# A hybrid encoder layer: level masks applied to the products of an inversion, the first up products in source order, split up weights in a pool of their own

## The chip, the cores and the metric

The kernel runs on one core of a Trainium2 chip. The metric is the device time of one execution in microseconds (us). Before the change it was 1162.3 us, the median of three runs (1160.35 to 1165.93). TensorE is called PE here, VectorE DVE, ScalarE ACT, GpSimd POOL and SyncE, which issues the DMAs, SP, as in the profile.

## The reference

One layer on 1024 tokens of width 1024: a combined input projection, a pooling group and a gated DeltaNet group side by side, an output projection, a squared-ReLU MLP of width 4096, and a last RMSNorm. What matters here, cut short:

```python
u = rms_norm(h, norm_mix)
proj = u @ w_in
pool_out = pool_mixer(proj[..., :P], w_pool, pool_scale)
qkv = causal_conv_silu(proj[..., P:P + 3 * G], conv_w)
gdn_out = gated_delta_net(...)          # lhs = I + strictly lower m; solves lhs against v and k
h = h + concatenate([pool_out, gdn_out]) @ w_out
u = rms_norm(h, norm_mlp)
h = h + square(relu(u @ w_up)) @ w_down
return rms_norm(h, norm_final)
```

## The kernel before

Tokens lie in eight tiles of 128, weights in blocks of 128 x 512. A float32 product is made of three matmuls on split operands: ACT casts an operand to its high half, DVE or POOL subtracts that to get the low half (`split`, line 951; `wh`/`wl` are the two halves of a weight, `th`/`tl` those of an activation operand), and `mm3` adds high x high, low x high and high x low.

**Order.** PE's instructions run in the order in which the program writes them. A planner interleaves dense work (input projection, convolution, output projection) with the chunk work by estimated due times. DVE, ACT, POOL and SP are put in order by the framework's scheduler, each engine by itself; within an engine everything then runs in that order, so a waiting instruction holds all that stand behind it.

**Chunks.** The DeltaNet works on 8 chunks of 128 tokens for 4 heads at once (tiles of 128 x 512). `invert` (line 573) inverts the unit lower triangular matrix by doubling: at level l, from 1 to 6, the blocks of size 2^l next to the diagonal are cut out of the matrix (`m1`, which is stored with ones on its diagonal) by a mask `lev[l]`, which has -1 in these blocks and 0 elsewhere. The cut-out `bl` is a POOL product (line 588), then PE multiplies it with the inverse so far (`px`), DVE adds the identity (`xx`, line 592), and PE multiplies `xx` with the inverse in both forms (`t`, `tt`). Level 0 takes two DVE operations (lines 578 and 579). At the same time DVE computes the convolution of the next projection tiles (`cy`, line 391) and POOL the low halves of input weights (`wl`, line 133).

**Up projection.** It goes by Strassen's scheme: 16 column pairs p of `w_up`, each with seven products i over half of the tokens and half of the depth. `up_load` (line 961) brings the 1 MB of a pair, `up_ready` (line 965) makes the sums of blocks for product i and splits them, `up_product` (line 1014) multiplies and evacuates, `combine` (line 1000) makes the seven operands of the down stage and stores them to DRAM (`hd`). The operands from the activations, TH[i] and TL[i], are made once: 1 and 2 by `turn_first`, the rest by `turn_second` (6 and 3), `operands_5`, `operands_7` and `operands_4` from the rows R[11], R[12], R[21], R[2], R[4], while the products of pairs 0 and 1 run. The list `order` (line 1048) says in which sequence; from pair 2 on it is 1, 6, 2, 5, 7, 3, 4. DVE makes the sums of blocks for pairs 0 and 1, POOL those of later pairs.

**Down projection.** Again seven products over the stored operands; `down_load` (line 1095) brings one or two weight blocks of 512 KB and an operand of `hd`, `down_ready` (line 1109) subtracts and splits. SP issues all loads and stores in one queue. Stores of the last pair are kept in the list `late` and issued after the first loads.

**Pools.** `ws` has the tags `raw` (3 buffers), `wh` and `wl` (5 each), used for nearly all split weights; `cp` has nine tiles "c" for the up stage's results; `wr2` holds the second weight of the down stage.

Of the kernel before, what the change touches and what calls it, by code (L numbers as in the profile page):

```python
# [28 lines left out]
def hybrid_trunk(ctx, tc, x, norm_mix, w_in, conv_w, w_pool, pool_scale, a_log, dt_bias,  # L29
# [218 lines left out]

    lev = []
    for l in range(7):  # L250
        b = 1 << l
        m = gp.tile([P, P], F16, name=f"lev{l}")
        nb = P // (2 * b)
        m3 = m.rearrange("p (n q) -> p n q", q=2 * b)
        G.memset(m3[:, :, 0:b], 0.0)
        G.memset(m3[:, :, b:2 * b], -1.0)

        G.affine_select(m3, m3, pattern=[[-2 * b, nb], [0, 2 * b]], compare_op=ALU.is_ge, fill=0.0, base=0,
                        channel_multiplier=1)
        G.affine_select(m3, m3, pattern=[[2 * b, nb], [0, 2 * b]], compare_op=ALU.is_gt, fill=0.0, base=b,  # L260
                        channel_multiplier=-1)
        lev.append(m)
# [310 lines left out]
    def invert(c, r):  # L573

        m1 = r["m1"]
        t, tt = gt("t", 3, F16), gt("tt", 3, F16)
        b0 = gt("bl", 2, F16)
        V.tensor_tensor(b0, m1, bc(lev[0]), op=ALU.mult)
        V.tensor_tensor(tt, b0, bc(ident_h), op=ALU.add)
        yield 1.0 * SLACK  # L580
        pt = bank()
        for h in range(NH):
            T.matmul(pt[:, h, :], tt[:, h, :], ident_h, start=True, stop=True)
        A.copy(t, pt)
        yield 0.9 * SLACK
        for l in range(1, 7):
            bl = gt("bl", 2, F16)
            G.tensor_tensor(bl, m1, bc(lev[l]), op=ALU.mult)  # L588
            px = bank()
            mm(px, bl, t)  # L590
            xx = gt("xx", dt=F16)
            V.tensor_tensor(xx, px, bc(ident), op=ALU.add)  # L592
# [260 lines left out]
    TH, TL = {}, {}  # L853
    u2c, u2p = opened(name="u2", bufs=1, side="right", reuse_waits="tile")
# [21 lines left out]
    wt[0] = [split_w(wov[:, k, :HALF], [P, HALF], V, *((w2p, "w2h", "w2l", 4, w2p, 6) if k >= 4 else (None, "wh", "wl", 5)))  # L876
# [6 lines left out]
    ys += norm_v(1, 1)  # L883
# [5 lines left out]
    R[12], R[2] = (u3(f"r{n}", F32) for n in (12, 2))  # L889
# [10 lines left out]

    def c_tile(nm):
        return cp.tile([P, HALF], F32, name=nm, tag="c")
# [30 lines left out]
    def operands_5():  # L933
        TH[5], TL[5] = (big_tile(f"t{m}5", [4, HALF], F32R) for m in "hl")
        parts_of(5, rows_of(11))

    def operands_7():

        for j in range(4):
            weighed(R[12][:, j, :], 4 + j, R[12][:, j, :])  # L940
        R[4] = [c_tile("r4") for _ in range(4)]
        for j in range(4):
            V.tensor_tensor(R[4][j], R[21][:, j, :], R[2][:, j, :], op=ALU.subtract)
        TH[7], TL[7] = u3("th7", F32R), big_tile("tl7", [4, HALF], F32R)
        parts_of(7, rows_of(12))
# [17 lines left out]

    def up_ready(p, i):

        r = raws[p]
        a11, a12, a21, a22 = r[:, :4, :P], r[:, 4:, :P], r[:, :4, P:], r[:, 4:, P:]
        eng = V if p < 2 else G
        if i == 1:
            eng.tensor_tensor(a21, a21, a22, op=ALU.add)  # L970
# [43 lines left out]
    def up_product(p, i, w):  # L1014
# [27 lines left out]
        else:  # L1042
# [5 lines left out]
    order = [(0, 1), (1, 1), lambda: turn_second(ys), (0, 2), (1, 2), operands_5, (0, 6), (1, 6), operands_7,  # L1048
             (0, 5), (1, 5), (0, 3), (1, 3), operands_4, (0, 7), (1, 7), (0, 4), (1, 4)]
# [20 lines left out]
    used = 0  # L1070
    for e in order:
# [11 lines left out]

    wrc, wr = opened(name="wr", bufs=4, side="right", reuse_waits="tile")
    xrc, xr = opened(name="xr", bufs=4, side="right", reuse_waits="tile")
    nfc, nf = opened(name="nf", bufs=1, side="right", reuse_waits="tile")
# [20 lines left out]

    def down_ready(i, s):
        x, w = raw_x.pop((i, s)), raw_w.pop((i, s))
        t = w[0]  # L1110
        if i == 5:
# [3 lines left out]
            V.tensor_tensor(t, w[0], w[1], op=ALU.subtract)  # L1115
# [52 lines left out]
    for n, (i, s) in enumerate(todo):  # L1168
# [3 lines left out]
        while late:  # L1172
            store(*late.pop(0))
# [50 lines left out]
```

## Time and profile before

| | |
|---|---|
| profiled execution | 1163.48 us |
| its span | 1161.8 us |
| mean granted TensorE clock | 0.987 |
| median of three runs | 1162.3 us |
| TensorE matmul busy | 1100.9 us, 95% |
| VectorE busy | 789.8 us, 68% |
| ScalarE busy | 601.5 us, 52% |
| GpSimd busy | 303.5 us, 26% |
| first of the up products starts | 515.0 us |
| 14th of the up products ends | 569.0 us |
| turn from up to down | about 843 us |

The span counts from the first to the last instruction. A row of a group has line, engine, operation, output and inputs, shape and count, then the busy time and the mean of one in ns, then the engine's idle time just before and what ended it. A row of the timeline has the start in us, the duration, and in brackets how long the engine stood idle before it and on what it waited. A wait row names who waited, on whom, the us in total, how often, and the longest. A row of a stretch begins with its bounds and its length.

### The profile page before, as it was taken

To read this page: it belongs to the slowest core of one execution; us is meant where nothing else is said; L and a number is where in the kernel's file an instruction comes from. 1 tells how busy PE (TensorE), PEld (TensorE's weight loads), DVE (VectorE), ACT (ScalarE), POOL (GpSimd) and SP (SyncE) were. 2 spreads that over 40 slices of the span, in tenths; PEclk is the share of its full clock that TensorE was granted. 3 is DMA by queue.
4 is the path that set the end of the run, shared out by engine and by line. 5 is a ranking of instruction groups with operands and counts; after the bars stand their busy time and mean duration, and the time that the engine had idled before them with its cause. 6 is when DMAs were issued, how large, how long until landed. Compare 5 with 4: busy or idle time off the path is not lost.

```text
span 1161.8 us, 15593 instructions
## 1 busy us (share of the span) xinstructions
PE 1100.9 (95%) x5606; PEld 893.6 (77%) x5606; DVE 789.8 (68%) x1240; ACT 601.5 (52%) x1113; POOL 303.5 (26%) x272
## 2 busy tenths in 40 slices
PE   6998999988998999997999999999989999999997
PEld 5776777767776787876788888888878888888886
DVE  5798688867879775669655555555465687466584
ACT  6666566564755555546554544454444334335353
POOL 6033365564755422000232313131100000000010
PEclk9999999998999999998999999999989999999999
DMA  5233121111223321120634343444298796265561
GB/s 161 82 98 121 56 59 41 55 52 40 55 60 118 109 65 55 37 73 18 209 133 166 128 162 137 156 144 146 89 373 298 270 393 224 94 199 194 186 215 73
DMA packets 93049, 155.24 MB, mean 134 GB/s; under 512 B 7782, under 2 KB 45739, under 8 KB 92971
## 3 DMA queue, kind: packets, MB, share of 16 engines
q1 hardware_dynamic: 92970, 154.24, 39.4%
q8 instruction: 44, 0.72, 0.3%
q14 instruction: 35, 0.28, 0.1%
HBM read 120.66 MB, written 33.55 MB: 133 GB/s over the span
## 4 chain that ended last, share of the span: by engine, by line
PE 70%; DVE 13%; ACT 3%; issue 2%; POOL 1%; DMA 1%; POOLq 0%; DVEq 0%; ACTq 0%
PE bank L44 52%; PE acc L44 18%; DVE cy L391 2%; DVE nxt L410 1%; DVE xx L592 1%; PE bank L48 1%; DVE wl L955 1%; DVE nxt L409 0%; DMA wu<-in_w_up_dram 0%; DVE r L908 0%; DVE tl L913 0%; ACT th L172 0%; DVE ul L173 0%; DMA raw<-in_w_out_dram 0%; DVE kn L533 0%
## 5 line engine op out<-in xcount | busy, mean ns | idle before, releaser
L44 PE MATMUL bank<-tl,wh 128*128 128x512 f32 x440 | 175.3, 398 | 5.8 <-DVE tl L913 5.8
L44 PE MATMUL bank<-th,wh 128*128 128x512 f32 x440 | 175.2, 398 | 0.3 <-ACT p L1024 0.3
L44 PE MATMUL bank<-th,wl 128*128 128x512 f32 x440 | 174.7, 397 | 0.0
L954 ACT CAST sh<-x 128x1024 fp32r<-128x1024 f32 x55 | 57.9, 1053 | 163.8 <-PE bank L44 155.1
L954 ACT CAST wh<-wu 128x512 fp32r<-128x512 f32 x110 | 68.0, 620 | 127.2 <-PE bank L44 120.7
L44 PE MATMUL bank<-th,sh 128*128 128x512 f32 x344 | 133.8, 389 | 0.0
L44 PE MATMUL bank<-th,sl 128*128 128x512 f32 x344 | 133.8, 389 | 0.0
L44 PE MATMUL bank<-tl,sh 128*128 128x512 f32 x344 | 133.8, 389 | 0.0
L44 PE MATMUL acc<-uh,wh 128*128 128x512 f32 x320 | 130.3, 407 | 1.6 <-DVE ul L173 0.9
L44 PE MATMUL acc<-ul,wh 128*128 128x512 f32 x320 | 129.3, 404 | 0.0
L44 PE MATMUL acc<-uh,wl 128*128 128x512 f32 x320 | 128.9, 403 | 0.0
L955 DVE TENSOR_TENSOR sl<-x,sh 128x1024 fp32r<-128x1024 f32 x55 | 67.3, 1224 | 89.5 <-ACT sh L954 89.4
L44 PEld LDWEIGHTS bank<-tl,wh 128*128 128x128 f32 x440 | 83.5, 190 | 26.8 <-DVE tl L913 7.8
L955 DVE TENSOR_TENSOR wl<-wu,wh 128x512 fp32r<-128x512 f32 x110 | 84.4, 768 | 28.4 <-ACT wh L954 26.8
L44 PEld LDWEIGHTS bank<-th,wh 128*128 128x128 f32 x440 | 83.3, 189 | 20.1 <-ACT p L1024 0.8
L44 PEld LDWEIGHTS bank<-th,wl 128*128 128x128 f32 x440 | 83.5, 190 | 19.3
L152 POOL TENSOR_TENSOR stf<-stf,mhalf 128x1 f32<-128x1 f32 x8 | 7.9, 998 | 327.3 <-DVE stf L1159 327.3
L588 POOL TENSOR_TENSOR bl<-m,lev 128x512 f16<-128x512 f16 x48 | 62.9, 1310 | 84.7 <-PE bank L44 72.3
L391 DVE SCALAR_TENSOR_TENSOR cy<-cr,cols,cy 128x512 f32<-128x512 f32 x72 | 73.2, 1022 | 9.0 <-ACT cy L389 8.4
L133 POOL TENSOR_TENSOR wl<-raw,wh 128x512 fp32r<-128x512 f32 x48 | 68.0, 1420 | 35.6 <-ACT wh L132 35.4
L44 PEld LDWEIGHTS bank<-th,sl 128*128 128x128 f32 x344 | 64.6, 188 | 13.5
L44 PEld LDWEIGHTS bank<-th,sh 128*128 128x128 f32 x344 | 64.5, 188 | 13.5
(336 smaller groups left out, 2365.4 us busy)
## 6 DMA issues: line engine op xcount, KB each, us to landing
w<-in_w_down_dram SPq DMA_DIRECT2D x72, 512.0 KB, 5.9
x<-hd SPq DMA_DIRECT2D x56, 512.0 KB, 3.5
raw<-in_w_in_dram SPq DMA_DIRECT2D x80, 256.0 KB, 2.7
wu<-in_w_up_dram SPq DMA_DIRECT2D x16, 1024.0 KB, 5.3
hd<-s SPq DMA_DIRECT2D x48, 256.0 KB, 2.3
raw<-in_w_out_dram SPq DMA_DIRECT2D x24, 256.0 KB, 2.7
xin<-in_x_dram SPq DMA_DIRECT2D x8, 512.0 KB, 5.3
h<-in_x_dram SPq DMA_DIRECT2D x8, 512.0 KB, 4.4
```

What stands on the lines that cost most here:

```text
L44: T0.matmul(out, lhsT, rhs, start=start, stop=stop, skip_group_check=goes_on)
L48: T0.transpose(out, in_, identity)
L133: eng.tensor_tensor(lo, raw, hi.bitcast(F32), op=ALU.subtract)
L152: last["rsqrt"] = G.tensor_tensor(s, s, mhalf[:, :n], op=ALU.pow)
L391: V.scalar_tensor_tensor(cy, cr[:, e:e + HALF], tap[e], cy, op0=ALU.mult, op1=ALU.add)
L410: V.tensor_tensor(nxt[:, n:], cur[:, n:], cur[:, :W - n], op=ALU.add)
L588: G.tensor_tensor(bl, m1, bc(lev[l]), op=ALU.mult)
L592: V.tensor_tensor(xx, px, bc(ident), op=ALU.add)
L954: A.copy(hi, src)
L955: V.tensor_tensor(lo, src, hi.bitcast(F32), op=ALU.subtract)
```

## The change

It has four parts.

1. **Masks.** `lev[l]` now has 1 on the diagonal as well (seven more POOL selects of 128 x 128), for l > 0 with the -1 in the mirrored blocks. Level 0 is one DVE product, `tt = m1 * lev[0]`. At the higher levels PE multiplies the whole `m1` with the inverse so far, and DVE multiplies the result by `lev[l]` instead of adding the identity. The 48 POOL products `bl` are gone.
2. **Up weights.** A pool `wp` of five buffers each for `wh` and `wl` is opened at the top of the memory; the split weights of the up products and half of those of the output projection go there. `cp` is gone, its tiles take the tags `wh` and `wl` of `ws` in turn. The first weight block of pairs 0 and 1 is loaded by itself (256 KB) and split during the output projection.
3. **First 14 up products.** From product (0, 1) to (1, 4) DVE and ACT, like PE, run in source order. Operand 5 with (0, 5) and (1, 5) comes ahead of operand 6, operand 3 is made by a function of its own, R[4] by POOL, and POOL also makes a12 - a11 and the block of product 7 for pairs 0 and 1.
4. **Down stage.** The second weight comes as two loads of 256 KB into the tags of `ws`, and subtractions with it are two of 128 x 512. The late stores are issued after the last of the first loads. The pools are opened in another order.

```diff
     lev = []
     for l in range(7):
...
-        G.memset(m3[:, :, 0:b], 0.0)
-        G.memset(m3[:, :, b:2 * b], -1.0)
+        first = l > 0
+        G.memset(m3[:, :, 0:b], -1.0 if first else 0.0)
+        G.memset(m3[:, :, b:2 * b], 0.0 if first else -1.0)
...
+        G.affine_select(m, m, pattern=[[-1, P]], compare_op=ALU.not_equal, fill=1.0, base=0, channel_multiplier=1)
         lev.append(m)
...
     def invert(c, r):
         t, tt = gt("t", 3, F16), gt("tt", 3, F16)
-        b0 = gt("bl", 2, F16)
-        V.tensor_tensor(b0, m1, bc(lev[0]), op=ALU.mult)
-        V.tensor_tensor(tt, b0, bc(ident_h), op=ALU.add)
+        V.tensor_tensor(tt, m1, bc(lev[0]), op=ALU.mult)
...
         for l in range(1, 7):
-            bl = gt("bl", 2, F16)
-            G.tensor_tensor(bl, m1, bc(lev[l]), op=ALU.mult)
             px = bank()
-            mm(px, bl, t)
+            mm(px, m1, t)
             xx = gt("xx", dt=F16)
-            V.tensor_tensor(xx, px, bc(ident), op=ALU.add)
+            V.tensor_tensor(xx, px, bc(lev[l]), op=ALU.mult)
...
+    wpc, wp = opened(name="wp", bufs=5, side="right", reuse_waits="tile")
...
-    cpc, cp = opened(name="cp", bufs=9, reuse_waits="tile")
...
     def c_tile(nm):
-        return cp.tile([P, HALF], F32, name=nm, tag="c")
+        nonlocal n_c
+        n_c += 1
+        return ws.tile([P, HALF], F32, name=nm, tag="wh" if n_c % 2 else "wl", bufs=5)
...
     def turn_second(ys):
+        TH[5], TL[5] = (big_tile(f"t{m}5", [4, HALF], F32R) for m in "hl")
         for k in range(KT):
             pt = turned_banks[k] = acc_bank() if k in (0, 1, 6, 7) else work_bank()
             turn(ys, k, pt)
...
+        for k in range(4):
+            A.activation(R[12][:, k, :], turned_banks[k], AF.Copy, scale=nmlp[:, k:k + 1])
+            weighed(R[11][:, k, :], k, R[11][:, k, :])
+        parts_of(5, rows_of(11))
+        for j in range(4):
+            weighed(R[2][:, j, :], 4 + j, R[11][:, j, :])
         parts_of(6, rows_of(2))
+
+    def operands_3():
+        R[4] = [c_tile("r4") for _ in range(4)]
         for j in range(4):
+            G.tensor_tensor(R[4][j], R[21][:, j, :], R[2][:, j, :], op=ALU.subtract)
             weigh(turned_banks[4 + j], 4 + j, TH[3][:, j, :], TL[3][:, j, :], nmlp)
...
+    def first_load(p):
+        r = ws.tile([P, 4, P], F32, name="raw", tag="raw", bufs=3)
+        nc.sync.dma_start(out=r, in_=wuv[:, :4, p * 256:p * 256 + P])
+        return split(r, [P, 4, P], wp if p else ws, "wh", "wl", 5)
...
-        eng = V if p < 2 else G
+        eng = V if p < 2 and i in (1, 6) else G
...
         if i == 1 and p < 2:
-            out = split(src, [P, 4, P], cp, "c", "c", 9)
+            out = first_parts[p]
         else:
-            out = split(src, [P, 4, P], ws, "wh", "wl", 5)
+            out = split(src, [P, 4, P], wp, "wh", "wl", 5)
         made2.add((p, i))
+        eng = G
...
-    order = [(0, 1), (1, 1), lambda: turn_second(ys), (0, 2), (1, 2), operands_5, (0, 6), (1, 6), operands_7,
-             (0, 5), (1, 5), (0, 3), (1, 3), operands_4, (0, 7), (1, 7), (0, 4), (1, 4)]
+    order = [(0, 1), (1, 1), lambda: turn_second(ys), (0, 2), (1, 2), operands_3, (0, 5), (1, 5), operands_7, (0, 6), (1, 6),
+             (0, 3), (1, 3), operands_4, (0, 7), (1, 7), (0, 4), (1, 4)]
+    N_FIRST = 14
...
+        if e == (0, 1):
+            get_ready(3)
+            in_order.enter_context(tc.manual_schedule(engines={mybir.EngineType.PE, mybir.EngineType.DVE, mybir.EngineType.Activation}))
+        elif used == N_FIRST:
+            in_order.close()
         if callable(e):
+            get_ready(used + 2 + LEAD)
             e()
...
-            t = (pools["w2"] if n else wr).tile(pair2, F32, name="w", tag="w")
+            if n:
+                t = [ws.tile([P, HALF], F32, name="w2", tag=tag, bufs=5) for tag in ("wh", "wl")]
+                for q in range(2):
+                    nc.sync.dma_start(out=t[q], in_=src[:, q, :])
...
-            V.tensor_tensor(t, w[0], w[1], op=ALU.subtract)
+            for q in range(2):
+                V.tensor_tensor(t[:, q, :], w[0][:, q, :], w[1][q], op=ALU.subtract)
...
-        while late:
-            store(*late.pop(0))
+        if late:
+            with tc.issue_after(last["load"].ins):
+                while late:
+                    store(*late.pop(0))
```

How it moves instructions is seen at three places. On DVE, at the inversion of the first chunk, level 0 before (names: `m` the matrix, `lev` the mask, `tt` the transposed inverse so far, `cy` and `cr` the convolution, `raw`/`wh`/`wl` an input weight and its halves):

```order
L550 TENSOR_TENSOR m_816<-m_816,ident_h 128x512
L386 COPY chalo<-cr 128x3
L578 TENSOR_TENSOR bl<-m_816,lev_239 128x512
L391 SCALAR_TENSOR_TENSOR cy<-cr,cols,cy 128x512
L579 TENSOR_TENSOR tt<-bl,ident_h 128x512
L133 TENSOR_TENSOR wl<-raw,wh 128x512
```

The same place with the change:

```order
L555 TENSOR_TENSOR m_837<-m_837,ident_h 128x512
L391 COPY chalo<-cr 128x3
L584 TENSOR_TENSOR tt<-m_837,lev_239 128x512
L396 SCALAR_TENSOR_TENSOR cy<-cr,cols,cy 128x512
L133 TENSOR_TENSOR wl<-raw,wh 128x512
```

`tt` stands one operation and one `cy` earlier; the rows of `xx` after it keep their places among the `cy`.

On DVE, at the start of the up projection before, around the operand of (0, 6) (`r_5783` is R[12], `r_5784` R[2], `r_5484` R[21], `r_6066` to `r_6069` R[4]; `tl_5788` and `tl_5786` are the low halves of operands 6 and 3):

```order
L908 SCALAR_TENSOR_TENSOR r_5783<-bank,cols,r_5783 128x512
L955 TENSOR_TENSOR wl<-wu,wh 128x512
L943 TENSOR_TENSOR r_6066<-r_5484,r_5784 128x512
L943 TENSOR_TENSOR r_6067<-r_5484,r_5784 128x512
L943 TENSOR_TENSOR r_6068<-r_5484,r_5784 128x512
L943 TENSOR_TENSOR r_6069<-r_5484,r_5784 128x512
L913 TENSOR_TENSOR tl_5788<-r_5784,th_5787 128x512
L173 SCALAR_TENSOR_TENSOR tl_5786<-acc,cols,th_5785 128x512
```

With the change, from the second turn on (`r_5397` is R[11], `r_5688` R[2]; `tl_5826` and `tl_5687` are the low halves of operands 5 and 6, `wu` the sum of blocks for product 6):

```order
L914 SCALAR_TENSOR_TENSOR r_5397<-acc,cols,r_5397 128x512 x2
L914 SCALAR_TENSOR_TENSOR r_5397<-bank,cols,r_5397 128x512 x2
L919 TENSOR_TENSOR tl_5826<-r_5397,th_5825 128x512 x4
L914 SCALAR_TENSOR_TENSOR r_5688<-bank,cols,r_5397 128x512 x2
L914 SCALAR_TENSOR_TENSOR r_5688<-acc,cols,r_5397 128x512 x2
L919 TENSOR_TENSOR tl_5687<-r_5688,th_5686 128x512 x4
L982 TENSOR_TENSOR wu<-wu 128x4x128
L959 TENSOR_TENSOR wl<-wu,wh 128x512
```

Operand 5 now stands ahead of operand 6, the four R[4] rows are gone from DVE, and R[12] and operand 3 come after operand 6.

On ACT, at the turn from up to down before (`v_8344`, `u_8304` and `p_8285` are results of pair 15, `x` and `w` the first operand and weight of the down stage):

```order
L998 ACTIVATE v_8344<-v_8344 128x512
L997 ACTIVATE u_8304<-u_8304 128x512
L998 ACTIVATE u_8304<-u_8304 128x512
L997 ACTIVATE p_8285<-p_8285 128x512
L998 ACTIVATE p_8285<-p_8285 128x512
L954 CAST wh<-x 128x512
L954 CAST wh<-w 128x512
```

With the change:

```order
L1011 ACTIVATE v_8260<-v_8260 128x512
L1010 ACTIVATE u_8220<-u_8220 128x512
L1011 ACTIVATE u_8220<-u_8220 128x512
L1010 ACTIVATE p_8201<-p_8201 128x512
L1011 ACTIVATE p_8201<-p_8201 128x512
L958 CAST wh<-x 128x512
L958 CAST wh<-w 128x512
```

Nothing moved here but the line numbers: the casts stand behind the relu and square of `p`, as before.

More of the change, by code (lines that the diff above doesn't have):

```diff
@@ L254, in hybrid_trunk @@
         m3 = m.rearrange("p (n q) -> p n q", q=2 * b)
-        G.memset(m3[:, :, 0:b], 0.0)
-        G.memset(m3[:, :, b:2 * b], -1.0)
-        G.affine_select(m3, m3, pattern=[[-2 * b, nb], [0, 2 * b]], compare_op=ALU.is_ge, fill=0.0, base=0,
+        first = l > 0
+        G.memset(m3[:, :, 0:b], -1.0 if first else 0.0)
+        G.memset(m3[:, :, b:2 * b], 0.0 if first else -1.0)
+        o = b if first else 0
+        G.affine_select(m3, m3, pattern=[[-2 * b, nb], [0, 2 * b]], compare_op=ALU.is_ge, fill=0.0, base=-o,
                         channel_multiplier=1)
-        G.affine_select(m3, m3, pattern=[[2 * b, nb], [0, 2 * b]], compare_op=ALU.is_gt, fill=0.0, base=b,
+        G.affine_select(m3, m3, pattern=[[2 * b, nb], [0, 2 * b]], compare_op=ALU.is_gt, fill=0.0, base=o + b,
                         channel_multiplier=-1)
+        G.affine_select(m, m, pattern=[[-1, P]], compare_op=ALU.not_equal, fill=1.0, base=0, channel_multiplier=1)
         lev.append(m)
@@ L875, in hybrid_trunk @@
     whole(out_proj(NT - 1, 1, wt[1], acc_bank, parts))
-    wt[0] = [split_w(wov[:, k, :HALF], [P, HALF], V, *((w2p, "w2h", "w2l", 4, w2p, 6) if k >= 4 else (None, "wh", "wl", 5)))
+    wt[0] = [split_w(wov[:, k, :HALF], [P, HALF], V, *((wp, "wh", "wl", 5, w2p, 6) if k >= 4 else (None, "wh", "wl", 5)))
              for k in range(KT)]
@@ L888, in hybrid_trunk @@
     u3 = lambda nm, dt: u3p.tile(ub, dt, name=nm, tag="u3", bufs=6)
-    R[12], R[2] = (u3(f"r{n}", F32) for n in (12, 2))
     TH[3], TL[3], TH[6], TL[6] = (u3(nm, F32R) for nm in ("th3", "tl3", "th6", "tl6"))
-    cpc, cp = opened(name="cp", bufs=9, reuse_waits="tile")
+    R[2], R[12] = (u3(f"r{n}", F32) for n in (2, 12))
     hdp = ctx.enter_context(tc.tile_pool(name="hd", bufs=1, space=bass.MemoryType.DRAM))
@@ L985, in hybrid_trunk @@
     late = []
+    first_parts = [first_load(p) for p in range(2)]
+    ys += norm_v(1, 1)
     def keep(p, i, t):
@@ L1070, in hybrid_trunk @@
     used = 0
+    in_order = ExitStack()
     for e in order:
+        if e == (0, 1):
[3 more added lines that the diff above has]
+            in_order.close()
         if callable(e):
+            get_ready(used + 2 + LEAD)
             e()
@@ L1079, in hybrid_trunk @@
     close(u2c)
+    nfc, nf = opened(name="nf", bufs=1, side="right", reuse_waits="tile")
+    xrc, xr = opened(name="xr", bufs=4, side="right", reuse_waits="tile")
     wrc, wr = opened(name="wr", bufs=4, side="right", reuse_waits="tile")
-    xrc, xr = opened(name="xr", bufs=4, side="right", reuse_waits="tile")
-    nfc, nf = opened(name="nf", bufs=1, side="right", reuse_waits="tile")
     spc, sp = opened(name="sp", bufs=3, side="right", reuse_waits="tile")
@@ L1097, in down_load @@
         for n, blk in enumerate(LOADS[i]):
-            if n and "w2" not in pools:
-                close(cpc)
-                pools["w2c"], pools["w2"] = opened(name="wr2", bufs=4, reuse_waits="tile")
-            t = (pools["w2"] if n else wr).tile(pair2, F32, name="w", tag="w")
             e, c = blk // 10 - 1, blk % 10 - 1
-            nc.sync.dma_start(out=t, in_=wdv[s][e][:, :, c * HALF:(c + 1) * HALF])
+            src = wdv[s][e][:, :, c * HALF:(c + 1) * HALF]
+            if n:
+                t = [ws.tile([P, HALF], F32, name="w2", tag=tag, bufs=5) for tag in ("wh", "wl")]
+                for q in range(2):
+                    nc.sync.dma_start(out=t[q], in_=src[:, q, :])
+            else:
+                t = wr.tile(pair2, F32, name="w", tag="w")
+                nc.sync.dma_start(out=t, in_=src)
             w.append(t)
         x = raw_x[(i, s)] = xr.tile(pair2, F32, name="x", tag="x")
-        nc.sync.dma_start(out=x, in_=hd[s][i])
+        last["load"] = nc.sync.dma_start(out=x, in_=hd[s][i])
     def down_ready(i, s):
@@ L1119, in down_ready @@
         elif i == 7:
-            V.tensor_tensor(t, w[0], w[1], op=ALU.subtract)
+            for q in range(2):
+                V.tensor_tensor(t[:, q, :], w[0][:, q, :], w[1][q], op=ALU.subtract)
         elif i == 4:
@@ L1123, in down_ready @@
         if (i, s) == (1, 0):
-            parts = [[split(o[:, q, :], [P, HALF], ws, "wh", "wl", 5) for o in (x, t)] for q in range(2)]
+            parts = [[split(o[:, q, :], [P, HALF], wp, "wh", "wl", 5) for o in (x, t)] for q in range(2)]
             return [(*parts[q][0], *parts[q][1]) for q in range(2)]
@@ L1188, in hybrid_trunk @@
             down_sums(i, t, sets, s == 0, s == NS - 1)
-    close(pools["w2c"])
     close(spc)
+    close(wrc)
+    close(xrc)
     close(nfc)
-    close(xrc)
-    close(wrc)
+    close(wpc)
     close(psgc)
```

14 lines of the change are left out of this document (1 added, 13 removed).

## The prediction

> **What bounds the kernel now.** I read the page's busy shares first, then PE's waits, then stretches of the span, then single operations where PE had waited.
>
> ```profile
> span 1161.8 us, 15593 instructions
> PE 1100.9 (95%) x5606; PEld 893.6 (77%) x5606; DVE 789.8 (68%) x1240; ACT 601.5 (52%) x1113; POOL 303.5 (26%) x272
> ```
>
> TensorE (PE) is the bound: it works 95% of the span. The change removes no matmul, so it can only save time in which PE stands still, 1161.8 - 1100.9 = 60.9 us by the page, or works at a lowered clock. Who makes it stand still is told by the waits (us in total, times, longest):
>
> ```profile
> PE bank L44 <- DVE xx L592: 15.3, 10, 3.0
> PE bank L48 <- DMA rnmix<-in_norm_mix_dram: 9.1, 1, 9.1
> PE bank L44 <- DVE tl L913: 5.8, 3, 5.3
> PE bank L44 <- ACT wh L954: 3.2, 1, 3.2
> ...
> PE bank L44 <- DVE c L955: 1.7, 2, 1.5
> ```
>
> The 9.1 us is the first load, which the change leaves alone. `xx` is in the inversion of the DeltaNet chunks, `c` and `tl` L913 at the start of the up projection, `wh` L954 at the turn from up to down. The stretches show how much each place can give (busy us of PE, PEld, DVE, ACT, POOL, then the granted TensorE clock, the DMA share and GB/s):
>
> ```profile
> 80.00:100.00 20.00, 16.27 (x97) 12.79 (x96) 15.25 (x27) 11.56 (x29) 9.16 (x7) 0.91 0.47 159
> 260.00:280.00 20.00, 17.03 (x115) 13.69 (x114) 17.70 (x27) 10.38 (x21) 12.65 (x9) 0.97 0.22 57
> 280.00:300.00 20.00, 19.16 (x116) 16.21 (x115) 13.82 (x25) 10.95 (x29) 8.98 (x7) 0.86 0.13 38
> 500.00:520.00 20.00, 18.47 (x80) 14.56 (x78) 11.18 (x21) 7.88 (x16) 2.51 (x4) 1.00 0.33 106
> 520.00:540.00 20.00, 14.34 (x74) 10.88 (x73) 20.00 (x33) 14.22 (x27) 0.00 (x0) 0.96 0.07 26
> 540.00:560.00 20.00, 19.39 (x75) 15.31 (x76) 15.81 (x26) 8.90 (x17) 0.48 (x1) 0.87 0.25 80
> 840.00:860.00 20.00, 16.76 (x61) 12.81 (x60) 13.72 (x16) 10.86 (x14) 0.00 (x0) 0.83 0.97 341
> 860.00:1140.00 280.00, 280.00 (x1237) 231.81 (x1236) 182.02 (x179) 114.41 (x132) 5.72 (x4) 1.00 0.67 231
> 580.00:840.00 260.00, 260.00 (x1119) 210.75 (x1118) 142.59 (x209) 127.60 (x209) 65.33 (x51) 1.00 0.40 140
> ```
>
> From 580 to 840 and from 860 to 1140 PE never stops: nothing there can be saved. Where it stopped longest the clock fell as well, as after the 3 us wait in the first chunk:
>
> ```profile
> 89.88 0.38 PE L44 MATMUL bank<-xx,tt 128*128 128x128 f16 x4 [2.99 <-DVE xx L592]
> ...
> 90.60 0.39 PE L44 MATMUL acc<-uh,wl 128*128 128x512 f32 x1
> 90.83 0.40 PE L44 MATMUL acc<-uh,wh 128*128 128x512 f32 x1
> ...
> 91.35 0.63 PE L44 MATMUL acc<-uh,wl 128*128 128x512 f32 x1
> ```
>
> Matmuls of 128x512 that took 0.39 and started 0.23 apart take 0.63. So a wait of 2 to 3 us costs itself and, by the clock column, some more: (1 - 0.91) x 20 = 1.8 us at 80, (0.03 + 0.14) x 20 = 3.4 at 260 to 300, (0.04 + 0.13) x 20 = 3.4 at 520 to 560, 0.17 x 20 = 3.4 at 840.
>
> The Trainium skill's "TensorE: Matmul & The Clock Gate" (What's actually happening) has the clock halve after an idle window of about 3.4 us; here it fell after 2.99, so the measured gap decides, and by the page no lowered clock would follow the shorter gaps of the slower rival below.
>
> **Masks: the 48 GpSimd products go.** The removed work and what runs beside it:
>
> ```profile
> L588 POOL TENSOR_TENSOR bl<-m,lev 128x512 f16<-128x512 f16 x48 | 62.9, 1310 | 84.7 <-PE bank L44 72.3
> L391 DVE SCALAR_TENSOR_TENSOR cy<-cr,cols,cy 128x512 f32<-128x512 f32 x72 | 73.2, 1022 | 9.0 <-ACT cy L389 8.4
> L133 POOL TENSOR_TENSOR wl<-raw,wh 128x512 fp32r<-128x512 f32 x48 | 68.0, 1420 | 35.6 <-ACT wh L132 35.4
> ...
> 72.49 0.75 DVE L391 SCALAR_TENSOR_TENSOR cy<-cr,cols,cy 128x512 f32<-128x512 f32 x1
> ...
> 79.48 1.40 POOL L588 TENSOR_TENSOR bl<-m,lev 128x512 f16<-128x512 f16 x1 [0.54 <-DVE chalo L386]
> 79.78 1.65 DVE L391 SCALAR_TENSOR_TENSOR cy<-cr,cols,cy 128x512 f32<-128x512 f32 x1
> ...
> L592 DVE TENSOR_TENSOR xx<-bank,ident x48: 671/682/693, 89.1 to 452.7; 128x512 f16<-128x512 f32 x48
> ```
>
> No wait of PE names `bl` itself: it is ready in time. But VectorE's `cy`, 0.75 us by itself, takes 1.65 when it starts while a `bl` runs, and `xx`, which reads PSUM, is never slower than 693 ns. Over 72 `cy` the excess is 73.2 - 72 x 0.75 = 19.2 us. `bl` is 62.9 of the 62.9 + 68.0 us of the two large GpSimd groups, 48%, so about 9.2 us of this excess is its doing. Beside it, `tt` is one VectorE operation where it was two (0.41 us less, 8 times: 3.3). VectorE thus gets back some 12.5 us in the chunks. `xx` keeps its count and shape, with another second operand. PE takes m1 in the place of `bl`, with the same tiles.
>
> The Trainium skill's "SBUF — State Buffer" (Who interferes with whom) says why: a VectorE operation with two SBUF inputs and a GpSimd one that reads SBUF exclude each other on a shared port, and the first to start keeps it. The 0.75 to 1.65 us of `cy` and the unmoved `xx` agree. Were each `bl` to hold VectorE for its whole 1.31 us, the page would give up to 62.9 us back, and the sum would go to its upper bound of 20.5; the mean of `cy` shows much less. The rule speaks for this step and against the next one, which gives GpSimd such operations.
>
> How much of 12.5 us arrives at PE? At most what PE loses by this path: 15.3, and the clock of the two places, 1.8 + 3.4, together **20.5**. At least nothing, or less by one longest wait (3.0) if VectorE's new order puts something else before `xx`. I take **-10**: nearer to what VectorE regains, since PE's waits sit where VectorE is late, and where the wait drops below 2 us the clock stays up too; a part is lost, because GpSimd's weight splits come earlier into the places left free and stretch VectorE as `bl` did. The seven further selects run on GpSimd at 20 to 27 us; a select took 0.3 to 0.7 us there:
>
> ```profile
> L260 POOL TENSOR_SCALAR_AFFINE_SELECT lev<-lev x7: 292/342/717, 19.1 to 26.1; 128x128 f16<-128x128 f16 x7
> ```
>
> The 7 x 0.34 = 2.4 us delay the weight splits behind them; no wait of PE names GpSimd there, so I count nothing, at most 2.4.
>
> **The first 14 up products.** PE's idle time from 500 to 560 is (20 - 18.47) + (20 - 14.34) + (20 - 19.39) = 7.8 us, and with 3.4 of clock 11.2 can be won at most. VectorE is full (20.00 of 20) just before the long wait:
>
> ```profile
> 537.19 2.49 DVE L943 TENSOR_TENSOR r<-r,r 128x512 f32<-128x512 f32 x4
> 539.60 0.68 DVE L913 TENSOR_TENSOR tl<-r,th 128x512 fp32r<-128x512 f32 x1
> 540.34 0.80 PE L44 MATMUL bank<-tl,wh 128*128 128x512 f32 x1 [5.27 <-DVE tl L913]
> ```
>
> Four subtractions for operand 4, which is needed last, stand ahead of the `tl` of operand 6. The change moves them to GpSimd, puts operand 5 with products (0,5), (1,5) ahead of 6, and splits the first weights early, which takes away the 1.5 us of `c`. After the second turn VectorE is still the bound. One operation of this kind starts some 0.62 us after the one before it (2.49 / 4), those that read PSUM 0.66; a product is 12 matmuls, 12 x 0.23 = 2.76 us. For operand 6 VectorE now does 20 of them: R11, operand 5, R2 and operand 6 (4 each), two sums and two weight splits, 20 x 0.65 = 13.0 us, while PE has four products, 11.0: it waits 2.0. From there to the end of operand 4 come 28 (operand 3, evacuations, splits, R7, operands 7 and 4), 28 x 0.64 = 17.9, beside six products, 16.6: 1.3. With nothing in VectorE's way PE waits 3.3 us: 3.3 - 11.2, about **-8**. But four R4 subtractions and four of a12 and a11, eight 128x512 GpSimd operations, now run beside VectorE's `tl`, whose two inputs are in SBUF. A pair from this stage:
>
> ```profile
> 559.52 1.30 POOL L970 TENSOR_TENSOR wu<-wu 128x512 f32<-128x512 f32 x1 [41.24 <-DMA wu<-in_w_up_dram]
> 560.09 1.28 DVE L955 TENSOR_TENSOR wl<-wu,wh 128x512 fp32r<-128x512 f32 x1 [1.31 <-ACT wh L954]
> ```
>
> `wl` takes 1.28 where `tl` took 0.68, 0.6 more; eight times is 4.8 us, and PE waits 3.3 + 4.8 = 8.1 again. But it does so in pieces, before operands 5, 6, 3, 7 and 4, that I estimate below 2 us each, after which the clock stays up (the 1.5 us of `c` lie in 500 to 520, clock 1.00): 8.1 - 11.2 = -3.1. Not every one of the eight will meet a `tl`, so I take **-4**, between -8 and 0.
>
> **The turn to down.** PE's wait here:
>
> ```profile
> 843.36 0.69 DVE L1043 TENSOR_TENSOR p<-bank,p 128x512 f32<-128x512 f32 x1
> 844.09 0.63 ACT L997 ACTIVATE p<-p 128x512 f32<-128x512 f32 x1 [1.50 <-DVE p L1043]
> 844.75 0.63 ACT L998 ACTIVATE p<-p 128x512 f32<-128x512 f32 x1
> 845.35 0.62 ACT L954 CAST wh<-x 128x512 fp32r<-128x512 f32 x1
> 845.88 0.61 ACT L954 CAST wh<-w 128x512 fp32r<-128x512 f32 x1
> 846.54 0.79 PE L44 MATMUL bank<-wh 128*128 128x512 f32 x1 [3.22 <-ACT wh L954]
> ```
>
> Loads come earlier in the change and the late stores behind them. But the first casts stand on ScalarE behind the relu and square of the last `p`, as before, and that waits for the end of the last up product. An earlier load finds the same queue: **0**, and at best 3.2 + 3.4 = 6.6.
>
> ```profile
> L955 DVE TENSOR_TENSOR sl<-x,sh 128x1024 fp32r<-128x1024 f32 x55 | 67.3, 1224 | 89.5 <-ACT sh L954 89.4
> ```
>
> In the down stage two 128x512 subtractions (0.69 each, as `p` above) stand for one of 128x1024 (1.22), and second weights come in two halves; PE is busy 280 of 280 us and VectorE 182, so it hides: 0. With the cover gone it would cost 0.16 us each time.
>
> **The sum**: the profiled execution took 1163.5 us, its span 1161.8 with 1.7 around it; it lies 1.2 over the median of 1162.3. 1163.5 - 10 - 4 = 1149.5, or 1148.3 beside the median; I say **1149**.
>
> **Rivals.** (a) *A bound is reached*: the turn's loads do what they ask for and its wait and clock go (1149.5 - 6.6 = 1143), or the masks give all that PE loses to `xx` (1163.5 - 20.5 - 4 = 1139). For it: `xx` is the one name behind the chunks' long waits. Against: ScalarE's order at the turn, and VectorE's 12.5 us. Chance 0.17. (b) *VectorE finds other waits*: its time comes back where PE doesn't wait, so that only the up start gains, or a little of both: -2 to -6, 1157 to 1161. That the masks do not do what they say is a part of this: PE names `xx`, never `bl`, and were `xx` late for the matmul before it, nothing would change. The 20.00 of 20 at 520 shows how full VectorE can be. Chance 0.20. (c) *Slower: the shared use moves instead of going.* The weight splits on GpSimd (68.0 us) fill the places of `bl`, so that the chunks gain nothing; and at the up start a GpSimd operation starts just ahead of a `tl` each time, which then waits out its 1.30 us: 8 x 1.30 = 10.4 in place of 4.8, 5.6 more, so +1.6 instead of -4; one gap of over 2.3 us brings the half clock back (0.13 x 20 = 2.6, as at 540): 1163.5 + 4.2 = 1168, and with 3.0 from a worse order in the chunks 1171. It decides once the mean of `cy` stays over 1000 ns and PE's wait for operand 6 exceeds 2.3 us. Against it: 62.9 us of GpSimd work are really gone. Chance 0.11. The forecast keeps 0.52.
>
> **Range and chances.** 1139 to 1164 takes in (a) and (b); (c) lies outside. About 0.5% is what a measurement of this kernel can tell from no change: under 1156.5 and over 1168.1 about the median. Faster: 0.52 + 0.17 + 0.04 of (b) = 0.73; slower: 0.08 of (c), its upper part; same: 0.16 of (b) + 0.03 of (c) = 0.19.
>
> **What would show it.** Masks: `cy` down from a mean of 1022 to about 900 ns, PE's waits for `xx` from 15.3 to under 8, the clock of 80 to 100 and 280 to 300 over 0.95. Up start: no wait over 2 us, clock over 0.95 from 520 to 560, the 14 products over 3 to 5 us sooner; the `tl` of operand 6 with a mean over 0.9 us, beside GpSimd's R4. Turn: PE's wait for `wh` still near 3 us. Wrong would be: `xx` waits unchanged with `cy` faster, a new wait longer than 2 us for operand 6 or 3, or a wait in the down stage.

## The result and the profile after

The changed kernel takes 1142.9 us (median of 4 runs, 1141.73 to 1143.28) against 1162.6 us before: 0.9827 of the time, 95% interval 0.9802 to 0.9852. The forecast was 1149, range 1139 to 1164. The profiled execution took 1142.87 us, its span 1140.8. The page of the changed kernel:

```profile
span 1140.8 us, 15548 instructions
PE 1091.9 (96%) x5606; PEld 890.2 (78%) x5606; DVE 762.5 (67%) x1240; ACT 599.9 (53%) x1113; POOL 257.1 (23%) x239
```

The matmuls are the same 5606, yet PE is busy 9.0 us less: part of the gain is no idle time at all. PE's waits:

```profile
PE bank L44 <- ACT wh L958: 4.5, 2, 3.1
PE bank L44 <- DVE v L1049: 4.3, 1, 4.3
PE bank L44 <- DVE xx L595: 3.2, 6, 0.8
```

The 15.3 us for `xx` are 3.2 now, none over 0.8. The 5.3 us for `tl` are gone, but there is a new wait of 4.3 us for `v`, and the one for `wh` at the turn is still there. The stretches (columns as in the prediction):

```profile
80.00:100.00 20.00, 19.16 (x124) 15.36 (x124) 16.44 (x34) 14.73 (x36) 5.21 (x4) 1.00 0.53 173
280.00:300.00 20.00, 18.09 (x111) 13.80 (x109) 16.45 (x24) 13.46 (x34) 13.12 (x10) 1.00 0.23 64
520.00:540.00 20.00, 17.20 (x65) 12.47 (x64) 16.26 (x26) 11.02 (x21) 3.37 (x3) 0.93 0.00 1
540.00:560.00 20.00, 17.07 (x68) 13.89 (x69) 14.43 (x21) 8.73 (x17) 8.97 (x5) 0.91 0.76 262
820.00:840.00 20.00, 16.75 (x61) 12.86 (x60) 13.45 (x16) 11.02 (x14) 0.00 (x0) 0.83 1.05 378
```

The clock stays up in these two stretches of the chunks and still falls at the up start and at the turn (now at 820). By the starts of the first and last matmuls of each stage the 21.0 us between the two profiled spans divide so:

| stage | before | after | difference |
|---|---|---|---|
| to the first up product | 515.0 | 494.5 | -20.5 |
| first 14 up products | 53.8 | 55.3 | +1.6 |
| other 98 up products | 274.2 | 270.4 | -3.8 |
| turn | 3.6 | 3.5 | -0.1 |
| down stage and tail | 315.3 | 317.1 | +1.8 |

### The profile page after: what moved, and what is told of

The parts are those of the page before. It is cut to its first block, busy times and chain, and to the rows that moved or that the text cites. A ratio compares the mean times of both kernels' runs of the same rounds, so it can differ in the third digit from the quotient of the medians.

```text
span 1140.8 us, 15548 instructions
## 1 busy us (share of the span) xinstructions
PE 1091.9 (96%) x5606; PEld 890.2 (78%) x5606; DVE 762.5 (67%) x1240; ACT 599.9 (53%) x1113; POOL 257.1 (23%) x239
## 4 chain that ended last, share of the span: by engine, by line
PE 68%; DVE 11%; ACT 3%; POOL 2%; DMA 2%; issue 2%; POOLq 0%; SPq 0%; DVEq 0%; ACTq 0%
PE bank L44 51%; PE acc L44 17%; DVE cy L396 2%; DMA x<-hd 1%; DVE tl L919 1%; PE bank L48 1%; DVE wl L959 1%; DVE r L914 1%; POOL rk L152 1%; DMA wu<-in_w_up_dram 0%; DMA w<-in_w_down_dram 0%; POOL wu L993 0%; DVE xx L595 0%; ACT wh L958 0%; POOL wl L133 0%
## 5 line engine op out<-in xcount | busy, mean ns | idle before, releaser
L44 PEld LDWEIGHTS bank<-tl,sh 128*128 128x128 f32 x344 | 64.6, 188 | 13.5
L44 PEld LDWEIGHTS acc<-uh,wh 128*128 128x128 f32 x320 | 60.3, 188 | 12.9 <-ACT cy L394 1.3
```

What stands on the lines that cost most here:

```text
L44: T0.matmul(out, lhsT, rhs, start=start, stop=stop, skip_group_check=goes_on)
```

## The experiments

### Masks alone

Only the masks of the change are put into the kernel before (the diffs of this part are cut to the lines that matter).

```diff
...
-            mm(px, bl, t)
+            mm(px, m1, t)
-            V.tensor_tensor(xx, px, bc(ident), op=ALU.add)
+            V.tensor_tensor(xx, px, bc(lev[l]), op=ALU.mult)
```

> The kernel before with the masks part alone. Theory A (the masks gave the whole gain of the chunks): the first up product starts near 494.5 us as in the changed kernel, not 515, the waits for xx fall to about 3 us, and the time is 1162.5 - 20.5 = 1142. Theory B (the early loads, the new pool and its places gave a part of it): the first up product starts at 500 us or later and the time is 1147 or more. Both expect the up stage itself as before: 54.0 us for the first 14 products and 0.233 us from matmul to matmul behind them.

It took 1144.1 us, 0.9851 of before (0.9835 to 0.9867). The first up product starts at 495.9 us, so the masks give 19.1 of the 20.5 us. In its waits the `xx` are as in the changed kernel, and `tl` as before the change:

```profile
PE bank L44 <- DVE tl L915: 5.8, 3, 5.3
PE bank L44 <- ACT wh L956: 3.3, 1, 3.3
PE bank L44 <- DVE xx L594: 3.2, 6, 0.8
```

### All but the masks

The reverse: the changed kernel with the old `lev` and `invert`.

> The changed kernel with the masks part undone. Theory A: the first up product starts at 513 to 516 us; the first 14 products take 55.6 us as in the changed kernel (1.6 more than before), the up stage behind them 3.8 us less than before; time 1160 to 1163. Theory B: the start stays nearer to 495 than to 515, time 1150 or less.

1161.4 us, 0.9998 of before (0.9984 to 1.0012): the other three parts together change nothing that can be measured. The up start takes 55.1 us, the other up products 270.5; the first up product starts at 511.3 us, 3.7 before 515.0, where at most 2.0 were expected. The profiled execution took 1159.5 us, 1.9 less than the median, and the one before the change about 1 more than its own, so most of the 3.7 need not be a gain.

### Products that nobody reads

The changed kernel with the 48 GpSimd products put back beside it.

```diff
         for l in range(1, 7):
+            bl = gt("bl", 2, F16)
+            G.tensor_tensor(bl, m1, bc(lev[l]), op=ALU.mult)
             px = bank()
             mm(px, m1, t)
```

> The changed kernel, and GpSimd still makes the 48 products of m1 and a mask, which nobody reads. Theory A1 (what cost the time was that these products run beside VectorE): at least half of the chunks' gain goes again, 1152 to 1163, mean of cy back from 905 to about 1000 ns, waits for xx over 8 us. Theory A2 (PE and VectorE had waited for the products themselves, or for the second operation of tt): the time stays at 1143 to 1146.

1160.9 us, 0.9986 of before (0.9972 to 0.9999): the gain is gone, though no instruction waits for a product. The first up product starts at 512.3 us again (17.7 of the 20.5 us lost). The groups of `cy` and `bl`:

```profile
L396 DVE SCALAR_TENSOR_TENSOR cy<-cr,cols,cy 128x512 f32<-128x512 f32 x72 | 73.1, 1018 | 5.5 <-ACT cy L394 4.8
L593 POOL TENSOR_TENSOR bl<-m,lev 128x512 f16<-128x512 f16 x48 | 65.2, 1384 | 5.2 <-DVE m L555 4.7 <-DVE chalo L391 0.5
```

and PE's wait:

```profile
PE bank L44 <- DVE xx L597: 12.7, 8, 6.4
```

`cy` is back at 1018 ns and `xx` is late again. Nor is GpSimd's own later work late: VectorE's waits for it are those of the changed kernel (7.6 us for `rk` and 2.6 for `m` in both). That settles it for theory A1: it was the running of the products beside VectorE, not a wait for them and not the second operation of `tt`.

### Weights and results exchanged in their places

```diff
-        return ws.tile([P, HALF], F32, name=nm, tag="wh" if n_c % 2 else "wl", bufs=5)
+        return wp.tile([P, HALF], F32, name=nm, tag="wh" if n_c % 2 else "wl", bufs=5)
-            out = split(src, [P, 4, P], wp, "wh", "wl", 5)
+            out = split(src, [P, 4, P], ws, "wh", "wl", 5)
```

> The changed kernel with the places of two things exchanged: split up weights from pair 2 on in the low tags (byte 23712 to 42144 of a partition), the results of the up stage in the pool at the top. Theory P (a matmul is slower when its operands lie low in the memory): from the 15th up product on 0.233 us from matmul to matmul in place of 0.227 to 0.231, the up stage 4 to 5 us longer, 1147 to 1148. Theory Q (the early or late writes of other engines or the order make the difference): the spacing stays, 1142 to 1144.

1160.7 us, 0.9982 of before (0.9968 to 0.9995), far from both theories, and for another reason in part: the second weights of the down stage lie in `ws` and now wait for the last up weights, so that PE waits 8.2 and 7.4 us at the turn. The up stage answers the question. Matmuls on record from 600 to 800 us, first before the change:

```profile
600.00:800.00 200.00, 200.00 (x861) 162.11 (x860) 111.59 (x164) 99.44 (x163) 53.20 (x42) 1.00 0.42 148
```

with the change:

```profile
600.00:800.00 200.00, 200.00 (x877) 164.25 (x876) 112.89 (x166) 101.46 (x167) 55.27 (x43) 1.00 0.42 146
```

and with the exchange:

```profile
600.00:800.00 200.00, 200.00 (x861) 162.46 (x860) 110.97 (x163) 99.46 (x164) 53.03 (x41) 1.00 0.42 146
```

PE is busy 200 of 200 us at clock 1.00 in all three, and does 877 matmuls in the changed kernel where the others do 861. The mean distance of their starts is 0.2328, 0.2285 and 0.2327 us. So where weights and results lie is worth 1176 x 0.0043 = 5.1 us of the up stage; the 3.8 in the table is less because a wait behind the 14 products takes 1.45 us where it took 0.33.

### DVE and ACT left to the scheduler at the up start

```diff
-            in_order.enter_context(tc.manual_schedule(engines={mybir.EngineType.PE, mybir.EngineType.DVE, mybir.EngineType.Activation}))
```

> The changed kernel with DVE and ACT left to the scheduler for the first 14 up products; their sequence and R4 on GpSimd stay. Theory A (source order makes the 4.3 us wait behind v L1049, because the evacuations of (0,7) stand behind operand 4, whose casts stand behind the relu and square of (1,3)): this wait goes or shrinks below 2 us, the 14 products take 50 to 53 us in place of 55.3, and the time is 1139 to 1142. Theory B (VectorE is simply full there, whatever the order): PE waits as long at another place, 55 us again or more, 1143 to 1147.

1136.4 us, 0.9779 of before (0.9761 to 0.9797), 6.5 less than the change: the 14 products take 49.7 us. The wait for `v` is gone; one for the `tl` of the second turn's operands is left:

```profile
516.55 0.80 PE L44 MATMUL bank<-tl,wh 128*128 128x512 f32 x1 [3.13 <-DVE tl L919]
```

The expectation blamed the casts of operand 4; the next run tests that alone.

### Operand 4 early

Still in source order; the casts of operand 4 are behind operand 7, its low halves behind (0, 3) and (1, 3).

```diff
...
-             (0, 3), (1, 3), operands_4, (0, 7), (1, 7), (0, 4), (1, 4)]
+             (0, 3), lambda: lows_4((0, 1)), (1, 3), lambda: lows_4((2, 3)), (0, 7), (1, 7), (0, 4), (1, 4)]
```

> The changed kernel, still in source order, but the casts of operand 4 directly behind operand 7 and its low halves two by two behind (0,3) and (1,3). Theory A: the wait behind v L1049 goes from 4.3 to under 1 us, with the lowered clock after it (1.8 us), and the 14 products take 49 to 51 us: 1137 to 1139. Theory B (VectorE is full): PE waits as much at (0,3) or (0,7), 55 us, 1143.

1140.8 us, 0.982 (0.9801 to 0.9839), and the 14 products take 55.4 us as with the change: theory A fell. The wait has the same length. Its PE and VectorE rows:

```profile
536.35 1.29 DVE L964 TENSOR_TENSOR wl<-wu,wh 128x512 fp32r<-128x512 f32 x2 [1.88 <-ACT wh L963]
...
541.32 0.69 DVE L964 TENSOR_TENSOR wl<-wu,wh 128x512 fp32r<-128x512 f32 x1 [1.86 <-ACT wh L963]
```

```profile
543.96 0.47 PE L44 MATMUL bank<-th,wh 128*128 128x512 f32 x1 [4.29 <-DVE v L1054]
```

VectorE is not full here either: it stands still twice, for ScalarE's cast of the next weight. What makes that late is seen in the changed kernel's ScalarE and VectorE:

```profile
533.48 0.63 ACT L1010 ACTIVATE u<-u 128x512 f32<-128x512 f32 x1 [3.66 <-DVE u L1053]
534.15 0.63 ACT L1011 ACTIVATE u<-u 128x512 f32<-128x512 f32 x1
534.69 0.60 ACT L958 CAST wh<-wu 128x512 fp32r<-128x512 f32 x1
```

```profile
532.77 0.68 DVE L1053 TENSOR_TENSOR u<-bank,u 128x512 f32<-128x512 f32 x1
535.32 0.69 DVE L959 TENSOR_TENSOR wl<-wu,wh 128x512 fp32r<-128x512 f32 x1 [1.87 <-ACT wh L958]
535.93 0.68 DVE L1053 TENSOR_TENSOR u<-bank,u 128x512 f32<-128x512 f32 x1
538.48 1.29 DVE L959 TENSOR_TENSOR wl<-wu,wh 128x512 fp32r<-128x512 f32 x2 [1.87 <-ACT wh L958]
```

In source order the evacuation of a product (`u`, VectorE), its relu and square (ScalarE), the cast of a later weight (ScalarE) and that weight's low half (VectorE) stand one behind the other on two engines, and the evacuation of the next product behind that. Each round costs VectorE 1.87 us, and the evacuations that PE needs come at the end. This chain is read from the trace: `order_off` shows that the wait goes with the order, but no run took away a single link.

### The first split of the down stage ahead of the last up product

```diff
     for e in order:
+        if e == (NPAIR - 1, 4):
+            down_first()
```

`down_first` loads the first weight and operand into a free tile and splits them into `wp`, so the loads, casts and subtractions all come earlier.

> The changed kernel, with the first operand and weight of the down stage loaded and split in the program ahead of the last up product, so that their four casts stand on ACT ahead of the relu and square of the last p. Theory A (the turn's wait is ACT's order): the wait of 3.13 us for wh falls below 0.7 us, the clock stays up, 6 to 6.5 us in all: 1136.5 to 1137. Theory B (it is the loads or the queue of SP): the wait stays near 3 us, 1142 to 1144.

1137.8 us, 0.9791 (0.9772 to 0.9811): 5.1 less than the change. PE is busy 20.00 of 20 us at the turn and the clock stays up:

```profile
820.00:840.00 20.00, 20.00 (x90) 16.57 (x89) 13.89 (x15) 11.38 (x14) 0.00 (x0) 1.00 1.02 377
```

### Both, and R4 on VectorE again

`off_turn` has both of these edits. `off_turn_r4` also gives R4 back to VectorE, written at operand 4:

```diff
...
     def operands_4():
+        R[4] = [c_tile("r4") for _ in range(4)]
+        for j in range(4):
+            V.tensor_tensor(R[4][j], R[21][:, j, :], R[2][:, j, :], op=ALU.subtract)
```

> Both of the earlier winners at once: DVE and ACT left to the scheduler at the first 14 up products, and the first split of the down stage ahead of the last up product. They are 300 us apart; theory A (independent): their gains add, 1142.9 - 6.5 - 5.1 = 1131.3, within 2 us. Theory B (the scheduler gives something back at one of them): 1134 or more.

> As off_turn, but the four R4 subtractions on VectorE again, written down at operand 4. Theory A (GpSimd's R4 stretches VectorE's tl beside it by as much as it saves): the wait of 3.1 us for tl L919 stays between 2 and 4 us and the time within 1 us of off_turn. Theory B (GpSimd's use of the port costs more): the wait falls below 1.5 us, 1.5 to 4 us less. Theory C (VectorE was the bound, taking R4 off it was right): the wait grows over 4 us, 2 us or more above off_turn.

The two took 1127.7 us (0.9701, 0.9685 to 0.9716) and 1125.4 us (0.9682, 0.9665 to 0.9698). The first is 3.6 us better than the sum of the gains. The traces show where: in `turn_early` the first up product starts at 497.0 us, 2.4 later than with the change (494.5) and before anything that was edited, and its 14 products take 0.6 longer; in `off_turn` it starts at 494.9. In the chunks of `turn_early` PE has waits like those of the changed kernel, but the clock falls more. From 350 to 400 us, with the change and in `turn_early`:

```profile
350.00:400.00 50.00, 46.96 (x312) 38.38 (x311) 33.27 (x64) 25.49 (x59) 12.30 (x9) 0.97 0.24 83
```

```profile
350.00:400.00 50.00, 46.97 (x300) 38.17 (x300) 33.28 (x63) 26.14 (x60) 12.30 (x9) 0.93 0.29 94
```

So the sum was too low because `turn_early` alone had lost some 3 us elsewhere; why the clock falls more in one of them stays open. In `off_turn_r4` the 14 products take 45.3 us in place of 49.7, the wait for `tl` is halved (1.54 us, just over what was expected) and the clock stays up: theory B.

```profile
516.96 0.50 PE L44 MATMUL bank<-tl,wh 128*128 128x512 f32 x1 [1.54 <-DVE tl L919]
```

```profile
496.70:542.20 45.50, 42.45 (x201) 34.91 (x200) 45.24 (x67) 30.55 (x55) 13.56 (x8) 1.00 0.23 77
```

This row ends where the 15th product starts. Two low halves of the second turn show what R4 had cost beside them, first in `off_turn`, then here:

```profile
510.60 2.88 DVE L919 TENSOR_TENSOR tl<-r,th 128x512 fp32r<-128x512 f32 x2
```

```profile
510.52 1.28 DVE L919 TENSOR_TENSOR tl<-r,th 128x512 fp32r<-128x512 f32 x2
```

Of the 4.4 us at the up start 2.3 arrive in the whole: the first up product starts 1.8 later in this profile, with the clock at 0.93 from 350 to 400. `off_turn_r4` is the fastest of all, faster than both kernels.

### Matmuls by themselves: place, offset, other engines

Three kernels, each run once, have nothing of the layer but runs of matmuls, to learn why the place of the weights matters.

> Nothing of the reference's computation but matmuls of 128x512 by themselves: runs of 24 that take their stationary and their moving operand from four places of the memory (s near byte 4,000, m near 78,000, u near 113,000, t near 176,000), first with all other engines quiet, then with ACT and DVE writing near 188,000. Theory P (the place itself): runs with an operand low in the memory start their matmuls 0.231 to 0.233 us apart, runs with both high 0.227, with nothing else going on. Theory Q (other engines' traffic in the same part of the memory): all 16 quiet runs have one spacing, 0.227.

All 16 quiet runs had starts 0.2267 us apart: theory P fell. The other engines' writes lay beside the warm-up here, so theory Q was not put to a test; and all operands had the same offset in a 2048-byte grid.

> Nothing of the reference's computation but runs of 24 matmuls of 128x512 in the up product's pattern, in five placings: A weights low, activations high (as before the change), B both high (as after it), C weights high, activations low, D weights low at the offset of the high ones, E weights high at the offset of the low ones. Seven stretches: q with the other engines quiet, then with ACT and DVE busy on low (el) and high (eh) bytes, GpSimd (gl, gh), and loads of 1 MB (dl, dh). Theory T (traffic of others beside the operand): A and C go to 0.230 or more in some of el, gl, dl and stay at 0.227 in q, B stays in all. Theory O (the offset): A and E are slow in all stretches, q too, B and D fast. Theory N (neither): 0.227 everywhere.

The first matmul of each run in the quiet stretch:

```profile
43.72 0.39 PE L68 MATMUL Aq<-th_high,wh_low 128*128 128x512 f32 x1
...
49.21 0.39 PE L68 MATMUL Bq<-th_high,wh_high 128*128 128x512 f32 x1
...
54.65 0.39 PE L68 MATMUL Cq<-th_low,wh_high 128*128 128x512 f32 x1
...
60.25 0.39 PE L68 MATMUL Dq<-th_high,wh_mid 128*128 128x512 f32 x1
...
65.71 0.39 PE L68 MATMUL Eq<-th_high,wh_odd 128*128 128x512 f32 x1
...
71.20 0.39 PE L68 MATMUL Ael<-th_high,wh_low 128*128 128x512 f32 x1
```

24 matmuls take 5.49 (A), 5.44 (B), 5.60 (C), 5.46 (D) and 5.49 us (E), and within 0.01 us the same in all other stretches: theory O. A and E have weights at byte 1184 of a 2048-byte grid and activations at 2016, one low, one high in the memory (bytes of the tile that holds the four blocks of a weight); B and D have both at 2016, again one high, one low; C has weights at 2016 and activations at 1184.

> Nothing of the reference's computation but runs of 48 matmuls of 128x512 in the up product's pattern, all other engines quiet, at the very bytes that the two kernels use: b1 and b5 products 1 and 5 before the change, a1, a5, a7, a3, a4 those after it, b1x and a1x the same with the next buffers of the weights, b1s and a1s with the weights shifted by 832 bytes to the other's offset, a5s with the activations of a5 shifted. Theory O (the bytes alone): b1 0.233, b5 0.231, a1 0.227, a5, a7 and a3 0.229 to 0.231, a4 0.228, as in the kernels; b1s goes to 0.228 or less, a1s to 0.229 or more. Theory T (bytes and other engines together): b1 stays at or under 0.229.

```profile
L54 PE MATMUL b1x<-lots 128*128 128x512 f32 x48 | 11.2, 391 | 0.0
...
L54 PE MATMUL a1s<-lots 128*128 128x512 f32 x48 | 11.1, 391 | 0.0
...
L54 PE MATMUL a1x<-lots 128*128 128x512 f32 x48 | 11.0, 389 | 0.0
L54 PE MATMUL b1s<-lots 128*128 128x512 f32 x48 | 11.0, 389 | 0.0
```

From start to start 48 matmuls of product 1 took 10.99 us at the bytes of before (0.2290 each) and 10.88 at those of after (0.2267). Shifting the weights by 832 bytes exchanges the two (b1s 10.88, a1s 10.99). Product 5 at the bytes of before, both operands at 1184, took 10.89. So the bytes alone make 0.0023 us of a product 1, where the two kernels differ by 0.0063 (0.2330 and 0.2267 in their up stages): not theory O's 0.233, but what theory T allows. The spacing of the changed kernel is what its bytes give by themselves, in products 1, 5, 7 and 4 within 0.0001 (5, with weights at 2016 and activations at 1184, takes 0.2333 in both); product 3 alone differs, 0.2275 by itself and 0.2302 in the kernel. The rest of the time before the change comes only with the whole kernel running, and what makes it stays open: GpSimd, loads, or ACT with DVE one at a time did not.

## Why the prediction was right or wrong

**The sum** held: -14 forecast, -19.6 measured, inside the range and faster as forecast. Part of that is luck, since two errors of opposite sign met: the masks gave 10.5 us more than was counted, the up start 5.6 less.

**Masks**: right in mechanism, mis-sized. The step was "I take -10: nearer to what VectorE regains". Measured are -20.5 to the first up product, the upper bound of 20.5, 19.1 of it by the masks alone. What was regained was taken from `cy` and `tt`, 9.2 + 3.3 = 12.5 us. But VectorE's whole busy time up to the first up product fell twice as much. Before the change, then with it:

```profile
0.00:515.00 515.00, 472.83 (x2886) 382.33 (x2887) 386.29 (x732) 305.64 (x679) 221.49 (x207) 0.99 0.25 75
```

```profile
0.00:494.50 494.50, 467.10 (x2886) 379.40 (x2887) 359.73 (x726) 305.09 (x680) 160.44 (x166) 1.00 0.26 80
```

386.3 - 359.7 = 26.6 us: `cy` gave 8.3 of it (73.2 to 64.9), level 0 of the inversion 6.1 (from 6.5 + 4.5 to 4.9, where 3.3 was counted), VectorE's other operations the rest. PE's idle time in the two rows fell by 14.8 us (42.2 to 27.4), 12.1 of it the waits for `xx`, and its busy time by 5.7, for the same 2886 matmuls at a higher clock, where the bound had 5.2. The discount for weight splits that fill the free places had no row behind it, and the waits for `xx` were shorter than it left them. The Trainium skill's page "SBUF — State Buffer" (Who interferes with whom), by which the sum would go to its upper bound, was nearer than the term taken; `dead_products` agrees with it, with `cy` at 1018 ns and 17.7 us.

**Up start**: wrong. Forecast -4, between -8 and 0; measured +1.6. PE's idle time came out as worked out, 8.2 us (55.5 - 47.3) for 8.1, but by luck: half of it is a wait that the working doesn't have. What failed is "pieces ... that I estimate below 2 us each, after which the clock stays up": one is 4.28 us, and the clock is 0.94 as before. The walk followed VectorE and PE and left out ScalarE, whose casts stand behind relu and square in source order. Without that order the same list of products gives 49.7 us, -4.0.

The second half of that step failed too: short pieces did not keep the clock up. After two of them matmuls of 0.39 us take 0.63:

```profile
517.06 0.50 PE L44 MATMUL bank<-th,wh 128*128 128x512 f32 x1 [1.33 <-ACT wh L958]
...
518.36 0.50 PE L44 MATMUL bank<-th,wl 128*128 128x512 f32 x1 [0.57 <-DVE wl L959]
...
519.77 0.63 PE L44 MATMUL bank<-tl,wh 128*128 128x512 f32 x1
```

Nor does one longer wait always lower it. The kernel before has this one, and its clock from 360 to 380 is 1.00:

```profile
362.53 0.38 PE L44 MATMUL bank<-xx,tt 128*128 128x128 f16 x4 [2.52 <-DVE xx L592]
```

So the length of one wait, 2 or 2.3 us, does not decide, as the prediction had it; what does is not shown here. GpSimd's R4 beside `tl` was foreseen, and its size for the four `tl` of operand 6 is here:

```profile
510.24 5.51 DVE L919 TENSOR_TENSOR tl<-r,th 128x512 fp32r<-128x512 f32 x4
```

against 2.49 us for the four of operand 5; taking R4 back gave 4.4 us of the 14 products in `off_turn_r4`.

**Turn**: right. Loads came earlier (the first at 815.2 us, 5.4 before the last up product ends, for 3.1 before the change), ScalarE waits for none of them, and the wait stayed, 3.13 for 3.22 us, with the same lowered clock (0.83). The last `p`, and the casts behind it:

```profile
822.03 0.63 ACT L1011 ACTIVATE p<-p 128x512 f32<-128x512 f32 x1
822.57 0.60 ACT L958 CAST wh<-x 128x512 fp32r<-128x512 f32 x1
```

`turn_early` brought these casts forward and won 5.1 us in the whole; by its trace the turn and what follows became 7.4 us shorter, 0.8 over the 6.6 that were named as the most.

**The rest, "0"**: wrong by two terms of opposite sign. Nobody looked for a faster matmul in the 260 us in which PE never stops (-5.1 us), since "nothing there can be saved" took a busy PE for a PE at its peak. And the down stage is 1.8 us longer; 1.19 of it is one wait of PE at 916.85 us for `h`, behind the halved subtractions on VectorE, which was read from the trace and not tried.

**Rivals**: (a) came about by its masks half, the bound of 20.5 reached, but not in the total of 1139, since the up start lost; (b) did not, with 3.2 us of waits for `xx` left; (c), slower, did not: the mean of `cy` fell to 905 ns.

## What to carry to other kernels

Work that nobody waits for can still be the most expensive in the kernel, if it runs beside an engine whose operations it stretches (here 48 products, 17.7 us): look at the stretched durations of all the neighbour's operations, not of one group. Before an order is fixed by hand on two engines that feed each other, follow the chain through both; a cast that stands behind another product's activation is a wait. And a busy share of 100% says that an engine has no gaps, not that its instructions run at their fastest.

## What was not expected of the hardware

In these runs a 128x512 matmul starts 0.2267 to 0.2275 us after the one before it when stationary and moving operand lie at the same offset of a 2048-byte grid (both at 2016, both at 1184, or both at 128), 0.229 with the stationary one at 1184 and the moving one at 2016, 0.2333 the other way round; low or high in the memory made at most 0.001, and other engines' work none. In the whole kernel before the change the weights at 1184 cost more, 0.233, for a reason that stays open.

The clock does not follow the length of PE's last wait alone. It fell after waits of 1.33 and 0.57 us within 3 us with the change, and stayed at 1.00 after one of 2.52 us before it.
